# Row-tile pairs in seven products, and when a block's end is written, in a two-layer encoder trunk

## The chip, the cores and the metric

The kernel runs on one core of one Trainium2 chip. Times are device microseconds of that core, as the median of several executions; a profiled execution has a time of its own. The engines are TensorE (PE; its weight loads are listed apart as PEld), VectorE (DVE), ScalarE (ACT), GpSimd (POOL) and SyncE (SP), which issues most transfers.

## The reference

Two layers over 256 tokens of width 2048, all in float32:

```python
for l in range(DEPTH):
    h = rmsnorm(x, norm_g[l])
    proj = h @ w_in[l]                       # 2048 x 7168 columns
    a_x, a_b, a_c, a_g, d_q, d_k, d_v, d_g, m_q, m_g = jnp.split(proj, offsets, axis=-1)
    y_a = short_gated_conv(a_x, a_b, a_c, conv_w[l], conv_b[l]) * jax.nn.silu(a_g)
    q = rmsnorm(d_q.reshape(b, s, DIFF_HEADS, 2, DIFF_HALF_DIM), diff_q_norm_g[l])
    k = rmsnorm(d_k.reshape(b, s, DIFF_HEADS, 2, DIFF_HALF_DIM), diff_k_norm_g[l])
    ...                                      # differential attention, 6 heads, and its gate
    mkv = rmsnorm(mem, mem_norm_g[l]) @ w_mem_kv[l]   # 256 memory tokens, 2048 x 1024
    ...                                      # attention into the memory, 4 heads, and its gate
    x = x + jnp.concatenate([y_a, y_d, y_m], axis=-1) @ w_out[l]
```

Nearly all the arithmetic is in the three products with `w_in`, `w_mem_kv` and `w_out`.

## The kernel before

**Products in three parts.** Each float32 operand is held as a high part `hi`, rounded to the type that TensorE takes, and a low part `lo`, what is left. A product is hi·hi + hi·lo + lo·hi, so each pair of a 128-row tile of weights (512 columns) and a tile of 128 tokens is three matmuls of 512 columns (`products`, called from L282).

**Blocks and chunks.** `block` computes 512 columns of a product for both token tiles: 16 row tiles, taken two at a time. Such a chunk loads 512 KB of weights on SP's queue into one of four `raw` tiles, casts them to `hi` on ScalarE (L271), subtracts for `lo` on VectorE (L272), and does 12 matmuls. There are four `hi` and four `lo` tiles, so the splitting can run up to four chunks ahead of TensorE. After each chunk `run_side` is called: it counts chunks and advances by one step every task whose due time has come. `later(g, n)` makes a task due n chunks on; a number that a task yields is the chunks until its next step. All other work (norms, turns, attention heads, convolution) is written as such tasks.

**Order.** A planner orders the program before it runs: by the order in which instructions are written, but it lets a later one go first when an earlier one is not ready by its own cost estimates. Instructions passed to `keep_in_program_order` (`pin` for short) stay in written order among themselves on their engine. On the chip each engine takes its list strictly in order.

**Pairs.** `seven` replaces two row tiles by two token tiles by two neighbouring blocks, eight tile products, by seven, of three matmuls each. It needs sums and differences of the tokens (`token_sums`: one add of 512 columns, four of 128, a cast and a subtract for their parts) and of the weights (four subtracts, L357; casts and `lo` of seven half tiles, L354), and four banks for the products that are shared (`x`, from the pools `ps_s` and `ps_t`). `joint` runs a block with such pairs put between its chunks at given `places`; the pairs also start the sums `far` of the next block, which then lacks those row tiles and is `near`'s partner. `near` and `far` together take all four `acc` banks. `collect` (L1041, L1045) and `gather` (L1068) add the shared products to both. Layer 0 has a joint at block 3 (partner 4) with one pair, layer 1 at block 1 (partner 2) with one, and the products with `w_out` two and three pairs.

**The attention blocks.** Blocks 0 to 2 of `w_in`'s attention columns hold queries and keys, 3 to 5 values and gates. In layer 0 they come in this order, after the product with the memory; in layer 1 twelve row tiles of blocks 3 and 0 are done first, then the rest of both, then 1, 2, 4, 5. At the end of a query or key block `normed` runs at once: sums of squares on ScalarE for 16 groups (L413), the mean and the root on GpSimd (L414, L185), and 16 multiplies of 64 columns on ScalarE (L421), which free the `acc` banks. Eight chunks later a task turns the sheet (L451), carries it through scratch memory in eight transfers, and splits it into `yT` (L509 to L519).

**The memory keys.** `keep_keys` copies the raw keys out of their banks; the task `mem_keys` norms them, and `keys` stores them to scratch (L821) and loads them back (L822), both on GpSimd's queue, and turns them on VectorE into `mkT` (L824, pinned).

Of the kernel before, what the change touches and what calls it, by code (L numbers as in the profile page):

```python
# [11 lines left out]
F32R = mybir.dt.float32r  # L12
I32 = mybir.dt.int32
AF = mybir.ActivationFunctionType
ALU = mybir.AluOpType
# [25 lines left out]
BIG = 3.0e38  # L41

# [7 lines left out]
def encoder(ctx: ExitStack, tc: tile.TileContext, x, mem, norm_g, w_in, conv_w, conv_b,  # L50
# [351 lines left out]
    def col(st, which, t):  # L402
        return st[:, which, t:t + 1]

    def normed_steps(acc, gs, st, home):

        ng, w = NB // gs, gs // B
        ss = small.tile([P, NT, ng], F32, tag=f"ss{ng}", name=nm("ss"))
        r = small.tile([P, NT, ng], F32, tag=f"rs{ng}", name=nm("rs"))
        for t in range(NT):  # L410
            for g in range(ng):
                sq = small.tile([P, gs], F32, tag="sq", name=nm("sq"), bufs=1)
                nc.scalar.activation(sq, acc[t][:, g * gs:(g + 1) * gs], AF.Square, accum_out=ss[:, t, g:g + 1])  # L413
            nc.gpsimd.tensor_scalar(ss[:, t], ss[:, t], 1.0 / gs, col(st, ET, t), ALU.mult, ALU.add)  # L414
            rsqrt(r[:, t], ss[:, t])
            yield 1
        both = home()
        for t in range(NT):
            for g in range(ng):
                j, b = divmod(g * w, NA)  # L420
                nc.scalar.activation(both[:, b:b + w, j, t], strips(acc[t][:, g * gs:(g + 1) * gs]), AF.Copy,  # L421
                                     scale=r[:, t, g:g + 1])
            yield 1
        return both

    def normed(*how):
        steps = normed_steps(*how)
        try:
            while True:
                next(steps)  # L430
        except StopIteration as end:
            return end.value
# [67 lines left out]
    def qk_T(l, yT, nat, q, k):  # L500

        whole = yield from turn_sheet(nat)
# [153 lines left out]

    def mem_pair(l, n, st):
        heads = (2 * n, 2 * n + 1)
        es = []
        for h in heads:  # L660
            while held["e"] == 2:
                yield 1
            held["e"] += 1
            es.append((yield from mem_scores(l, h, st)))
            yield 2
        yield 4
# [142 lines left out]
    def mem_keys(l, kraw):  # L809

        nat = yield from normed_steps([kraw[:, t] for t in range(NT)], P, stm[0], sheets("v"))
        yield 6
        yield from keys(l, nat)

    def keys(l, nat):
# [7 lines left out]
        yield 8  # L823
# [8 lines left out]
    class Memory:  # L832
# [5 lines left out]
        def load(self, s):  # L838
            if s in self.raw or s in self.parts or s >= DEPTH * KT + KT // CK:
                return  # L840
            l, k = divmod(s, KT)
            self.raw[s] = raw_tile()
            if l == DEPTH:
                pin(nc.sync.dma_start(self.raw[s], x_row_tiles(w_in[0], k * CK)[:, :, C_D:C_D + NB]))
                return
# [169 lines left out]
    for l in range(DEPTH):  # L1015
# [17 lines left out]
        def joint(b, places, summed, home):  # L1033
# [18 lines left out]
            def pair_at(n):  # L1052
                def run(near):
                    rows = lambda k: x_row_tiles(w_in[l], k, 1)[:, 0, C_D + b * NB:C_D + (b + 2) * NB]
                    seven(xT, 2 * n, summed[n], rows, near, far, x, n == 0, n == len(places) - 1,
                          ((tmp, ("sh", "e")[n]),) * 2, lambda: None, ((tmp, "e"), (keep, "mga"))[l])
# [6 lines left out]
                    between={c: pair_at(n) for n, c in enumerate(places)})  # L1063
# [13 lines left out]
        near_b, far_b, places, tags, home = ((3, 4, (10,), ("bgx",), "bgT"), (1, 2, (8,), ("bgT",), "bgx"))[l]  # L1077
        far, summed = None, []
        for b in order:
            if l == 0 and b == near_b - 1:  # L1080
                summed = [x_sums(n, tags[n]) for n in range(len(places))]
            if b in begun:
                acc = x_block([(C_D + b * NB, NB)], ALLK[-QT:], acc=begun[b])
                if b == 3:
                    for n in range(len(places)):
                        summed.append(x_sums(n, tags[n]))
            elif b == near_b:
                acc, far, us = joint(b, places, summed, home)
                acc = gather(acc, us[0:2])
            elif b == far_b:  # L1090
                acc = x_block([(C_D + b * NB, NB)], ALLK[2 * len(places):], acc=far, opened=(True, False))
                acc = gather(acc, us[2:4])
            else:
                acc = x_block([(C_D + b * NB, NB)], ready=m.ready if l == 0 and b == order[0] else None)
# [10 lines left out]
            if b < 3:  # L1105
                tasks.append(later(qk_T(l, yT, normed(acc, HALF, st, sheets(("mqT", "mga", "e")[b])),
                                 (0, 0, 4) if b == 0 else (0, 4, 2) if b == 1 else None,
                                 (256, 0, 2) if b == 1 else (0, 2, 4) if b == 2 else None), 8))
            else:
                for t in range(NT):  # L1110
                    if b == 3:
                        nc.scalar.activation(v[:, t, 0:NB], acc[t], AF.Copy, scale=col(st, R, t))
                    elif b == 4:
                        nc.scalar.activation(v[:, t, NB:768], acc[t][:, 0:256], AF.Copy, scale=col(st, R, t))
                        silu2(ga[:, t, 0:256], acc[t][:, 256:512], st, t)
                    else:
                        silu2(ga[:, t, 256:768], acc[t], st, t)
# [5 lines left out]
        def turn_mq(nat):  # L1123
# [4 lines left out]
        tasks.append(later(turn_mq(normed(acc, P, st, sheets("bgx"))), 8))  # L1128
# [207 lines left out]
```

## Time and profile before

| | |
|---|---|
| median of 3 executions | 918.17 us (917.14 to 918.65) |
| the profiled execution | 920.46 us |
| its span, first to last instruction | 918.7 us |
| TensorE busy | 910.9 us (99%) |
| VectorE busy | 638.8 us (70%) |
| ScalarE busy | 589.0 us (64%) |
| GpSimd busy | 125.3 us (14%) |
| moved by transfers | 215.18 MB, 234 GB/s |

A group's row gives line, engine, operation, what is written from what, shape, count, then busy time in us, mean ns of one, and the idle time of the engine ahead of it with what ended it. A row of the timeline or of the chain begins with the start and the duration in us; in the timeline a bracket gives idle time and its releaser.

### The profile page before, as it was taken

Reading aid. Unit: us, or ns where it says so; the run is one execution under the profiler, and the core shown is the slowest. Engines: PE = TensorE matmul, PEld = TensorE weight load, DVE = VectorE, ACT = ScalarE, POOL = GpSimd, SP = SyncE. Lnnn points to the kernel's source line nnn. Section 1 sums busy time; section 2 is a strip of 40 time slices with the busy share of each in tenths; the row PEclk is TensorE's granted clock in tenths of the full one; section 3 lists DMA queues with packets and bytes.
Section 4 is the critical chain, followed back from the end, with each engine's and each line's share of the span. In section 5 each row is a group of like instructions: output and inputs, shape, how many; then the busy total and the mean of one; then the engine's idle time right before and its main releaser. Section 6 shows DMA issues by size and latency. Waiting matters only on the chain.

```text
span 918.7 us, 12662 instructions
## 1 busy us (share of the span) xinstructions
PE 910.9 (99%) x4203; PEld 752.3 (82%) x4203; DVE 638.8 (70%) x877; ACT 589.0 (64%) x1226; POOL 125.3 (14%) x187
## 2 busy tenths in 40 slices
PE   9999999999999999999999999999999999999998
PEld 6887787888888888888888888888888888888887
DVE  5557645677658658677689666667658678588786
ACT  6679776757767656545557558787667666546352
POOL 2376142200031010000000202221032010000000
PEclk9999999999999999999999999999999999999999
DMA  8898777876777989978776874988768998968842
GB/s 288 284 266 252 236 227 226 255 215 221 222 212 205 256 228 262 265 234 246 254 228 226 259 251 130 277 241 238 223 183 230 266 271 248 271 206 241 281 154 92
DMA packets 244051, 215.18 MB, mean 234 GB/s; under 512 B 131977, under 2 KB 171721, under 8 KB 243985
## 3 DMA queue, kind: packets, MB, share of 16 engines
q1 hardware_dynamic: 239008, 208.71, 76.1%
q0 software_dynamic: 3776, 4.59, 1.9%
q10 hardware_dynamic: 1200, 1.07, 0.3%
q8 instruction: 33, 0.54, 0.2%
q14 instruction: 34, 0.27, 0.1%
HBM read 193.30 MB, written 21.00 MB: 233 GB/s over the span
## 4 chain that ended last, share of the span: by engine, by line
PE 88%; DMA 5%; ACT 2%; DVE 2%; POOL 2%; issue 1%; DVEq 0%; ACTq 0%; POOLq 0%
PE acc L282 80%; PE x L328 2%; DMA raw<-in_w_mem_kv_dram 2%; DMA raw<-in_w_in_dram 2%; PE acc L328 2%; PE po L489 1%; PE s L579 1%; DMA sh<-kd 1%; DVE lo L869 1%; PE po L706 1%; DVE xf L743 1%; ACT hi L271 1%; ACT sq L413 1%; POOL rs L185 1%; ACT sh L421 0%
## 5 line engine op out<-in xcount | busy, mean ns | idle before, releaser
L282 PE MATMUL acc<-hi,xT 128*128 128x512 f32 x1760 | 550.4, 390 | 0.0
L272 DVE TENSOR_TENSOR lo<-raw,hi 128x1024 fp32r<-128x1024 f32 x266 | 323.6, 1221 | 171.0 <-ACT hi L271 166.1
L271 ACT CAST hi<-raw 128x1024 fp32r<-128x1024 f32 x266 | 278.4, 1052 | 189.0 <-PE acc L282 138.2
L282 PEld LDWEIGHTS acc<-hi,xT 128*128 128x128 f32 x1760 | 330.3, 188 | 68.6
L282 PE MATMUL acc<-lo,xT 128*128 128x512 f32 x880 | 343.1, 390 | 2.0 <-DVE lo L272 1.6
L282 PEld LDWEIGHTS acc<-lo,xT 128*128 128x128 f32 x880 | 165.2, 188 | 36.3 <-DVE lo L272 2.0
L282 PE MATMUL acc<-hi,yT 128*128 128x512 f32 (+1 forms) x432 | 134.2, 388 | 0.0
L282 PEld LDWEIGHTS acc<-hi,yT 128*128 128x128 f32 x432 | 81.0, 188 | 16.7
L282 PE MATMUL acc<-lo,yT 128*128 128x512 f32 x216 | 83.7, 388 | 0.0
L282 PE MATMUL acc<-hi,memT 128*128 128x512 f32 x248 | 78.7, 393 | 0.0
L869 DVE SCALAR_TENSOR_TENSOR lo<-raw,cva,hi 128x1024 fp32r<-128x1024 f32 (+1 forms) x34 | 40.7, 1218 | 24.8 <-ACT hi L868 24.8
L282 PEld LDWEIGHTS acc<-hi,memT 128*128 128x128 f32 x248 | 46.1, 188 | 9.5
L282 PE MATMUL acc<-lo,memT 128*128 128x512 f32 x124 | 48.6, 392 | 0.7 <-DVE lo L869 0.7
L282 PEld LDWEIGHTS acc<-lo,yT 128*128 128x128 f32 x216 | 40.6, 188 | 8.4
L868 ACT ACTIVATE hi<-raw,cva 128x1024 fp32r<-128x1024 f32 (+1 forms) x34 | 36.5, 1098 | 7.6 <-DMA raw<-in_w_mem_kv_dram 7.0
L354 ACT CAST hi<-wide 128x1024 fp32r<-128x1024 f32 x21 | 22.0, 1056 | 18.1 <-DVE wide L357 7.4
L185 POOL TENSOR_TENSOR rs<-ss,root 128x8 f32<-128x8 f32 (+1 forms) x20 | 31.7, 1583 | 1.7
L354 DVE TENSOR_TENSOR lo<-wide,hi 128x1024 fp32r<-128x1024 f32 x21 | 25.4, 1221 | 8.4 <-ACT hi L354 8.2
L414 POOL TENSOR_SCALAR ss<-ss,st 128x8 f32<-128x8 f32 (+1 forms) x16 | 10.5, 654 | 137.4 <-ACT sq L413 137.4
L282 PEld LDWEIGHTS acc<-lo,memT 128*128 128x128 f32 x124 | 23.3, 188 | 6.6 <-DVE lo L869 1.8
L596 ACT ACTIVATE e<-e,mx 128x256 f32<-128x256 f32 x48 | 23.8, 497 | 6.7 <-DVE mx L591 6.0
L394 POOL TENSOR_SCALAR stt<-ssum 128x2 f32<-128x2 f32 x3 | 1.5, 507 | 187.3 <-DVE ssum L770 187.3
(207 smaller groups left out, 858.6 us busy)
## 6 DMA issues: line engine op xcount, KB each, us to landing
raw<-in_w_in_dram SPq DMA_DIRECT2D x188, 512.0 KB, 4.9
raw<-in_w_out_dram SPq DMA_DIRECT2D x54, 512.0 KB, 4.6
raw<-in_w_in_dram SPq DMA_DIRECT2D x64, 256.0 KB, 4.1
raw<-in_w_mem_kv_dram SPq DMA_DIRECT2D x30, 512.0 KB, 6.1
d<-sh SPq DMA_DIRECT2D x88, 128.0 KB, 4.4
sh<-d SPq DMA_DIRECT2D x72, 128.0 KB, 3.8
wide<-in_w_out_dram SPq DMA_DIRECT2D x10, 512.0 KB, 5.9
xs<-in_x_dram SPq DMA_DIRECT2D x4, 512.0 KB, 6.5
```

The source lines that it names most:

```text
L185: nc.gpsimd.tensor_tensor(r, t, root[:, 0:n], ALU.pow)
L271: nc.scalar.copy(hi, raw)
L272: nc.vector.tensor_tensor(lo_, raw, hi.bitcast(F32), ALU.subtract)
L282: i = nc.tensor.matmul(acc, left, right, start=start, stop=stop)
L328: nc.tensor.matmul(acc, left[a], right[b], start=first and i == 0, stop=last and i == 2)
L354: return ((hi, pin(nc.scalar.copy(hi, src))), (lo, pin(nc.vector.tensor_tensor(lo, src, hi.bitcast(F32), ALU.subtract))))
L413: nc.scalar.activation(sq, acc[t][:, g * gs:(g + 1) * gs], AF.Square, accum_out=ss[:, t, g:g + 1])
L414: nc.gpsimd.tensor_scalar(ss[:, t], ss[:, t], 1.0 / gs, col(st, ET, t), ALU.mult, ALU.add)
L489: nc.tensor.matmul(po[:, t, :], eT[:, i, t, k, :], v[:, k, h * P:(h + 1) * P], start=k == 0, stop=k == NT - 1)
L596: nc.scalar.activation(e[:, c, i], e[:, c, i], AF.Exp, bias=mx[:, c, i:i + 1], scale=-1.0, accum_out=sm[:, c, i:i + 1])
L868: both = (nc.scalar.activation(hi[:, j], raw[:, j], AF.Copy, scale=g), nc.vector.scalar_tensor_tensor(lo[:, j], raw[:, j], g, hi[:, j].bit ...
L869: nc.vector.scalar_tensor_tensor(lo[:, j], raw[:, j], g, hi[:, j].bitcast(F32), ALU.mult, ALU.subtract))
```

## The change

- `normed_steps` does its squares in steps of four groups for the 64-wide heads, and its multiplies as one VectorE `tensor_tensor` for each token tile, with the factor broadcast, in place of 16 (or 4) on ScalarE. `normed` is gone: the norms of blocks 0 to 2 and of the memory queries are steps of a task.
- The ends of the six attention blocks (norm, or copies and gates, and `gather` ahead of them) are tasks due two chunks after their block.
- Layer 0 has two joints, at blocks 1 and 3, with two pairs each at places 4, 8 and 6, 10; layer 1 has one, at block 1, with two pairs at 6, 10. The pairs' landing places and the tile for the first half tile's parts are set for each pair.
- The token sums stand in row tiles 12 to 15 of `yT`, which the memory heads fill later, and are made by a task during block 0 (layer 0) or after block 3 (layer 1).
- The memory keys' chain waits 5 chunks for 6 ahead of its store, but its norm's steps are two chunks longer; the turn is 11 chunks after the load for 8. Layer 0's sheet is in tile `bgT`, layer 1's in `v` as before.
- The second pair of memory heads waits until the first has its scores; FIRST is 0 and changes nothing.

```diff
@@ normed_steps
                 nc.scalar.activation(sq, acc[t][:, g * gs:(g + 1) * gs], AF.Square, accum_out=ss[:, t, g:g + 1])
+                if g % 4 == 3 and g + 1 < ng:
+                    yield 1
...
         for t in range(NT):
-            for g in range(ng):
-                j, b = divmod(g * w, NA)
-                nc.scalar.activation(both[:, b:b + w, j, t], strips(acc[t][:, g * gs:(g + 1) * gs]), AF.Copy,
-                                     scale=r[:, t, g:g + 1])
-            yield 1
+            to = both[:, :, :, t].rearrange("p (g b) j c -> p j g b c", b=w)
+            of = acc[t].rearrange("p (j g b c) -> p j g b c", g=NA // w, b=w, c=B)
+            nc.vector.tensor_tensor(to, of, r[:, t].rearrange("p (j g) -> p j g", g=NA // w).unsqueeze(3).unsqueeze(4)
+                                    .to_broadcast([P, NB // P, NA // w, w, B]), ALU.mult)
+            yield 2
@@ qk_T
-    def qk_T(l, yT, nat, q, k):
+    def qk_T(l, yT, get, st, home, q, k):
+        nat = yield from normed_steps(get(), HALF, st, home)
         whole = yield from turn_sheet(nat)
@@ mem_pair
+        while n > 0 and (l, n - 1) not in begun_pairs:
+            yield 1
@@ mem_keys, keys
-        nat = yield from normed_steps([kraw[:, t] for t in range(NT)], P, stm[0], sheets("v"))
-        yield 6
+        nat = yield from normed_steps([kraw[:, t] for t in range(NT)], P, stm[0], sheets(("bgT", "v")[l]))
+        yield 5
         yield from keys(l, nat)
...
-        yield 8
+        yield 11
@@ the layer's loop
-        def x_sums(n, tag):
-            home = keep.tile([P, 2, 4, P], F32R, tag=tag, name=nm("sums"))
-            for _ in token_sums(xT, 2 * n, home):
-                pass
-            return home
+        def x_sums(n):
+            home = yT[:, :, KT - QT + 2 * n:KT - QT + 2 * (n + 1)].rearrange("p two k (h r) -> p two (k h) r", r=P)
+            summed.append(home)
+            yield from token_sums(xT, 2 * n, home)
...
-        near_b, far_b, places, tags, home = ((3, 4, (10,), ("bgx",), "bgT"), (1, 2, (8,), ("bgT",), "bgx"))[l]
+        turned, raw, late = ((tmp, "sh"),) * 2, ((tmp, "e"),) * 2, ((keep, "v"), (keep, "ga"))
+        mga, bgx = (keep, "mga"), (keep, "bgx")
+        joints = ({1: ((4, 8), (turned, raw), (mga,) * 2, "bgT"), 3: ((6, 10), (late, turned), (bgx,) * 2, "bgT")} if l == 0
+                  else {1: ((6, 10), (raw, turned), (mga,) * 2, "bgx")})
...
+            if l == 0 and b == 0:
+                tasks.append(later(all_x_sums(), 1))
+            finish = None
             if b in begun:
                 acc = x_block([(C_D + b * NB, NB)], ALLK[-QT:], acc=begun[b])
                 if b == 3:
-                    for n in range(len(places)):
-                        summed.append(x_sums(n, tags[n]))
-            elif b == near_b:
-                acc, far, us = joint(b, places, summed, home)
-                acc = gather(acc, us[0:2])
+                    tasks.append(later(all_x_sums(), 1))
+            elif b in joints:
+                places = joints[b][0]
+                acc, far, us = joint(b, *joints[b])
+                finish = us[0:2]
...
+            def sums_of(acc=acc, us=finish):
+                return gather(acc, us) if us else acc
...
-                tasks.append(later(qk_T(l, yT, normed(acc, HALF, st, sheets(("mqT", "mga", "e")[b])),
+                tasks.append(later(qk_T(l, yT, sums_of, st, sheets(("mqT", "mga", "e")[b]),
...
-                                 (256, 0, 2) if b == 1 else (0, 2, 4) if b == 2 else None), 8))
+                                 (256, 0, 2) if b == 1 else (0, 2, 4) if b == 2 else None), 2))
...
+                tasks.append(later(leave(b, sums_of, v, ga), 2))
...
-        tasks.append(later(turn_mq(normed(acc, P, st, sheets("bgx"))), 8))
+        tasks.append(later(turn_mq(normed_steps(acc, P, st, sheets("bgx"))), 0))
```

More of the change, by code (lines that the diff above doesn't have):

```diff
@@ L41 @@
 BIG = 3.0e38
+FIRST = 0
 C_X, C_B, C_C, C_G = 0, 768, 1536, 2304
@@ L665, in mem_pair @@
             yield 2
+        begun_pairs.add((l, n))
         yield 4
@@ L838, in load @@
         def load(self, s):
-            if s in self.raw or s in self.parts or s >= DEPTH * KT + KT // CK:
+            if s in self.raw or s in self.parts or s >= DEPTH * KT + (KT - FIRST) // CK:
                 return
@@ L843, in load @@
             if l == DEPTH:
-                pin(nc.sync.dma_start(self.raw[s], x_row_tiles(w_in[0], k * CK)[:, :, C_D:C_D + NB]))
+                pin(nc.sync.dma_start(self.raw[s], x_row_tiles(w_in[0], FIRST + k * CK)[:, :, C_D:C_D + NB]))
                 return
@@ L1025, in x_block, with joint @@
             return block(xT, w_in[l], cols, order, rows=x_row_tiles, **how)
[L1027 to L1033 removed]
+        def x_sums(n):
+            home = yT[:, :, KT - QT + 2 * n:KT - QT + 2 * (n + 1)].rearrange("p two k (h r) -> p two (k h) r", r=P)
+            summed.append(home)
+            yield from token_sums(xT, 2 * n, home)
+        def joint(b, places, homes, singles, home, **how):
             near, far = accumulators(), accumulators()
@@ L1062, in joint @@
             x_block([(C_D + b * NB, NB)], ALLK[2 * len(places):], acc=near, opened=(False, False),
-                    between={c: pair_at(n) for n, c in enumerate(places)})
+                    between={c: pair_at(n) for n, c in enumerate(places)}, **how)
             return near, far, us
@@ L1076, in encoder, with all_x_sums @@
         begun = {b: x_block([(C_D + b * NB, NB)], ALLK[:-QT], more=True) for b in order[:2]} if l > 0 else {}
-        near_b, far_b, places, tags, home = ((3, 4, (10,), ("bgx",), "bgT"), (1, 2, (8,), ("bgT",), "bgx"))[l]
+        turned, raw, late = ((tmp, "sh"),) * 2, ((tmp, "e"),) * 2, ((keep, "v"), (keep, "ga"))
+        mga, bgx = (keep, "mga"), (keep, "bgx")
+        joints = ({1: ((4, 8), (turned, raw), (mga,) * 2, "bgT"), 3: ((6, 10), (late, turned), (bgx,) * 2, "bgT")} if l == 0
+                  else {1: ((6, 10), (raw, turned), (mga,) * 2, "bgx")})
         far, summed = None, []
+        def all_x_sums():
+            for n in range(2):
+                yield from x_sums(n)
+                yield 1
         for b in order:
-            if l == 0 and b == near_b - 1:
-                summed = [x_sums(n, tags[n]) for n in range(len(places))]
+            if l == 0 and b == 0:
+                tasks.append(later(all_x_sums(), 1))
+            finish = None
             if b in begun:
@@ L1121, in encoder, with turn_mq @@
         acc = x_block([(C_M, NB)])
-        def turn_mq(nat):
+        def turn_mq(steps):
+            nat = yield from steps
+            yield 1
             yield from turn_sheet(nat, mqT)
```

35 lines of the change are left out of this document (16 added, 19 removed).

## The prediction

> **What bounds the kernel now.** I read the page first: shares of busy time, then the chain that ended last.
>
> ```profile
> span 918.7 us, 12662 instructions
> PE 910.9 (99%) x4203; PEld 752.3 (82%) x4203; DVE 638.8 (70%) x877; ACT 589.0 (64%) x1226; POOL 125.3 (14%) x187
> PE 88%; DMA 5%; ACT 2%; DVE 2%; POOL 2%; issue 1%; DVEq 0%; ACTq 0%; POOLq 0%
> ```
>
> TensorE is busy all the time and is 88% of the chain. A busy TensorE can still run slowly, so I looked at the pace next, in the chain in order of time:
>
> ```profile
> 403.77 65.32 PE acc L282 x288
> ```
>
> 65.32 us for 288 matmuls of 512 columns is 0.227 us each. The 390 ns that the groups give as the mean of one is overlapped time; a matmul that goes away is worth 0.227 us. Then TensorE's waits, and its timeline around the three stops on VectorE's `lo`:
>
> ```profile
> PE acc L282 <- DVE lo L272: 1.6, 1, 1.6
> PE acc L282 <- DVE lo L869: 0.7, 2, 0.5
> PE acc L282 <- DVE lo L861: 0.5, 1, 0.5
> ...
> 100.99 0.84 PE L282 MATMUL acc<-hi,xT 128*128 128x512 f32 x3
> 102.29 0.50 PE L282 MATMUL acc<-lo,xT 128*128 128x512 f32 x1 [0.46 <-DVE lo L861]
> 104.47 0.84 PE L282 MATMUL acc<-hi,xT 128*128 128x512 f32 x3
> 105.33 0.50 PE L282 MATMUL acc<-lo,xT 128*128 128x512 f32 x1
> 148.31 0.61 PE L282 MATMUL acc<-hi,xT 128*128 128x512 f32 x2
> 150.48 0.50 PE L282 MATMUL acc<-lo,xT 128*128 128x512 f32 x1 [1.56 <-DVE lo L272]
> ```
>
> By start times: three matmuls from 100.99 should be followed at 101.67, and the next starts at 102.29 (0.62 lost); from 104.47 at 105.15, and it is 105.33 (0.18); two from 148.31 at 148.76, and it is 150.48 (1.72). Each restart takes 0.50 where a running matmul takes 0.39, another 0.11 each. Together 2.85 us. VectorE's timeline tells whose fault that is:
>
> ```profile
> 99.88 1.25 DVE L824 STREAM_TRANSPOSE mkT<-sh 128x1024 f32<-128x1024 f32 x1 [4.76 <-DMA sh<-kd]
> ...
> 141.21 0.29 DVE L339 TENSOR_TENSOR sums<-sums,f 128x128 f32<-128x128 f32 x1
> 147.87 1.25 DVE L824 STREAM_TRANSPOSE mkT<-sh 128x1024 f32<-128x1024 f32 x1 [6.38 <-DMA sh<-kd]
> ```
>
> Both times the turn of the memory keys (L824) stood at the head of VectorE's queue before its load had landed. The `lo` halves of the weights were queued behind it, and TensorE ran through its stock.
>
> **The change, part by part.** *Pairs.* A row-tile pair does 21 matmuls in place of 24. There were one joint block with one pair in each layer; now layer 0 has two joints of two pairs and layer 1 one of two: 6 for 2, four more, 4 x 3 x 0.227 = 2.72 us less on TensorE, wherever it is fed.
>
> *What a pair costs VectorE.* Rows of the groups by shape:
>
> ```profile
> L272 DVE TENSOR_TENSOR lo<-raw,hi 128x1024 fp32r<-128x1024 f32 x266 | 323.6, 1221 | 171.0 <-ACT hi L271 166.1 <-DMA raw<-in_w_in_dram 1.5 <-DMA sh<-d 1.2
> L357 DVE TENSOR_TENSOR wide<-wide 128x512 f32<-128x512 f32 x14 | 9.7, 692 | 0.5
> L354 DVE TENSOR_TENSOR one<-wide,one 128x512 fp32r<-128x512 f32 x7 | 4.8, 684 | 2.0 <-ACT one L354 2.0
> L1068 DVE TENSOR_TENSOR u<-acc,u 128x512 f32<-128x512 f32 x8 | 5.2, 675 | 0.0
> L421 ACT ACTIVATE sh<-acc,rs 128x64 f32<-128x64 f32 x64 | 14.5, 335 | 5.0 <-POOL rs L185 5.0
> L343 DVE TENSOR_TENSOR sums<-sums,sums 128x512 fp32r<-128x512 f32 x7 | 4.8, 685 | 0.9 <-ACT sums L342 0.9
> ```
>
> A pair asks 0.68 (`one`) + 3 x 1.22 (as long as L272's) + 4 x 0.69 (differences) = 7.1 us of VectorE; the two chunks that it replaces ask 2 x 1.22 = 2.44. So each new pair is 4.7 us more for VectorE while TensorE's share falls from 5.46 to 4.77. ScalarE gets three half-size casts more, and the loads move the same 1 MB on SP's queue in two transfers of 512 KB, so neither sets anything new.
>
> *Layer 0's window.* Three of the four new pairs fall between the first x block and the fourth, so I summed VectorE there, and beside it the two nearest rows, layer 1's joint and the end of the last product with three pairs:
>
> ```profile
> 98.50:207.00 108.50, 106.46 (x466) 86.85 (x465) 68.84 (x68) 76.98 (x220) 21.04 (x21) 1.00 0.77 230
> 876.00:899.00 23.00, 23.00 (x103) 18.89 (x102) 22.08 (x24) 14.70 (x17) 0.00 (x0) 1.00 0.38 121
> 553.00:583.00 30.00, 30.00 (x133) 24.74 (x132) 22.18 (x24) 23.04 (x75) 5.98 (x6) 1.00 0.54 162
> ```
>
> (The fields are length, then busy time of TensorE, its weight loads, VectorE, ScalarE, GpSimd.) VectorE had 68.8 us. To come: 3 pairs x 4.7 = 14.0; a second `collect`, four adds of the kind of L1068, 2.7; four more `gather` adds, 2.7; eight norm multiplies that leave ScalarE, 8 x 0.69 = 5.5; one more set of token sums, 2.4 (L343's split and an add of its size at 0.68 each, four quarter-size adds like L339's at 0.28). That is 96.1 us. TensorE will want 108.5 - 3 x 0.68 - 2.85 = 103.6 us for the same blocks: VectorE at 93%, with 7.5 us to lose. The three pairs at 876 to 899 ran at 22.08 of 23.0, 96%, and TensorE was busy for all 23.0. So a stretch this dense can be fed if the stock is full at its start. What the one pair of layer 0 lost itself is in TensorE's timeline:
>
> ```profile
> 182.62 0.39 PE L328 MATMUL acc<-hi,sums 128*128 128x512 f32 x1
> 182.98 0.50 PE L328 MATMUL acc<-hi,xT 128*128 128x512 f32 x1
> ```
>
> 0.36 between two starts, 0.13 too much, and 0.11 for the restart: 0.24. I charge each of layer 0's three new pairs with that, 0.7 us in all, and layer 1's with nothing, where VectorE goes from 22.2 to 22.2 + 4.7 + 1.4 = 28.3 of 29.3. The bounds are 0, as at 876, and what VectorE would run over if its waits stayed:
>
> ```profile
> DVE lo L272 <- ACT hi L271: 17.8, 12, 3.2
> DVE mkT L824 <- DMA sh<-kd: 11.1, 2, 6.4
> DVE yT L519 <- ACT yT L518: 2.7, 1, 2.7
> DVE lo L354 <- ACT hi L354: 2.4, 1, 2.4
> DVE one L354 <- ACT one L354: 2.0, 1, 2.0
> DVE lo L861 <- ACT hi L861: 2.0, 2, 1.5
> DVE yT L510 <- ACT yT L509: 1.8, 1, 1.8
> DVE xT L757 <- ACT xT L756: 1.2, 1, 1.2
> DVE sums L343 <- ACT sums L342: 0.9, 1, 0.9
> ```
>
> Without the keys' 11.1 and the 17.8 behind ScalarE's casts these are 13.0 us. If all remained, and ScalarE's 5.0 us behind `rs` (L421 above) came over with the multiplies, VectorE would need 96.1 + 18.0 = 114.1 us, 10.5 too many. I take the low end, because most of the 13.0 are waits on a ScalarE that loses the small L421 of three blocks here, 3 x 16 x 0.335 = 16 us, against some 5 us of new casts.
>
> *The keys' chain.* In steps of a chunk (12 matmuls, 2.73 us), the first store to scratch moves from 10 to 11 after the chain's first step and the turn from 8 to 11 behind the load's issue. POOL's store and load go one chunk later, the turn four. Three chunks more between load and turn are 8.2 us, against waits of 4.76 and 6.38. So L824 should find its data, and the 2.85 us go. What was behind it (`lo`) runs straight on; what waits for mkT, the memory heads, comes long after. The `v` tile is held until then, 147.87 + 4 x 2.73 = 158.8, and the first pair of the second joint wants it as a landing place. That pair reaches TensorE at about 98.5 + 21.9 + 25.9 + 16.4 + 8.2 = 170.9 (a whole block, a joint of six chunks and two pairs, its partner's six chunks, three chunks more), 12 us later: nothing, or up to 1 us if the load of some 6 us is crowded. Bounds: all of it, or nothing if the load moves as far as the turn.
>
> *Block ends.* The squares and multiplies are written two chunks later and in smaller steps, so the casts for the next chunks go first. They now hand the banks over late, and a joint's `far` sums need two banks of the block before. ScalarE's and GpSimd's rows for the first block's end (it ended at 98.5 + 21.9 = 120.4) give the times:
>
> ```profile
> 124.93 1.64 POOL L185 TENSOR_TENSOR rs<-ss,root 128x8 f32<-128x8 f32 x1
> 127.69 1.16 ACT L421 ACTIVATE sh<-acc,rs 128x64 f32<-128x64 f32 x5
> ```
>
> Before, the first bank was free at 128.85. Now one VectorE multiply behind `rs` frees it at 126.57 + 0.7 = 127.3; the first joint's first pair starts two chunks after 120.4, at 125.9, and asks for it as its third product, six matmuls on, at 127.2. If the multiply comes no sooner than the old eight plus two chunks, 134.3, the pair does its other six products first (4.1 us) and TensorE stands 134.3 - 125.9 - 4.1 = 4.3 us. I take nothing: VectorE reaches it as soon as `rs` lands unless it is behind.
>
> The query and key turns go from 8 to 10 chunks behind their block, with their eight scratch transfers on SP. Tightest is layer 1, where the first keys' split and the first scores stand so:
>
> ```profile
> 614.85 0.74 DVE L519 SCALAR_TENSOR_TENSOR yT<-sh,kgain,yT 128x512 fp32r<-128x512 f32 x1
> 622.42 1.62 PE s L579 x24
> ```
>
> Two chunks later is 621.1, still ahead of 622.4. If it is later yet, x blocks fill TensorE: nothing; the whole pair would slip by a chunk. The token sums' new home, the guard in the memory pairs, FIRST = 0 and the memory queries' steps issue nothing new on the path.
>
> *A rule to weigh.* TensorE's weight loads are busy 82%, its matmuls 99%. The Trainium skill, Perfetto Trace Analysis, section Identifying the Most-Contended Engine, holds matmul busy time to be a bad measure of headroom and weight-load busy time a good one; by that TensorE would have 18% of slack, and the 2.72 us might be absorbed. The trace disagrees where the pace is 0.227 us over 288 matmuls with no wait in between.
>
> **The sum.** The profiled execution took 920.46 us, 918.7 of span and 1.8 around it; it lies 2.3 over the median of 918.17. 920.46 - 2.72 - 2.85 + 0.7 = 915.6, which stands to a median of 913.3.
>
> **Rivals.**
> - *VectorE becomes the bound in layer 0.* Place: 98 to 207. From 7.5 us of waits on, each further one is a microsecond of TensorE. With the 18.0 above: 918.2 - 2.7 - 2.85 + 10.5 = 923.1, and with some 2 us of stock at the start (it was used up at 102 and is refilled) 921. For it: 93%, and every wait on `rs` now stands in VectorE's queue. Against it: 96% without a stop at 876. Slower.
> - *Late banks.* 4.3 us in the first joint and that less one chunk (2.7), 1.6, in layer 1's, whose first pair stands a chunk further on: 913.3 + 5.9 = 919.2. For it: the order written. Against it: the multiply is one instruction, and free to run early.
> - *The keys' waits only move.* 913.3 + 2.85 = 916.2. Against it: 8.2 us exceed both waits.
> - *The matmuls saved are absorbed.* 913.3 + 2.72 = 916.0. The pace speaks against it.
> - *Cleaner than I charge.* No loss at the pairs, and the 0.7 behind L869 gone as well, since ScalarE's small multiplies ahead of it go: 911.9.
>
> **How the numbers follow.** Forecast 0.54 (its own range 912.4 to 915.6), cleaner 0.08, keys 0.08, absorbed 0.04, late banks 0.15, VectorE 0.11. No change that can be told is within 0.2%, 916.3 to 920.0. Faster gets the first two and most of the next two, 0.70; the same the rest of those and the banks, 0.19; slower 0.11. The range leaves out the VectorE rival above and the best part of the cleaner case below: 911.7 to 919.4.
>
> **What would show it.** 12 fewer matmuls of 512 columns; L328 with 231 matmuls for 147; L824 without idle time ahead of it and no TensorE stop at 102 or 150; twenty VectorE multiplies of some 0.69 us where L421 was. VectorE near 96 us in layer 0's window. Wrong if TensorE's waits list shows more than 3 us behind `lo` of L354 or L272, or behind a multiply that frees a bank.

## The result and the profile after

The changed kernel takes 923.29 us (median of four, 923.03 to 923.83) against 917.78 for the kernel before on the same chip (917.14 to 918.65): a ratio of 1.006, 95% interval 1.0043 to 1.0078. It is slower; 913.3 had been forecast. The profiled execution took 923.83 us. Line numbers after the change are one higher (the matmul of the blocks is L283, ScalarE's cast L272, VectorE's subtraction L273, the pair's half tiles L355, its differences L358, its matmuls L329); the new multiply is L424, the sum of squares L414, the mean L417, the root `rs` L186.

The head of the page and the chain by engine, after:

```profile
span 922.0 us, 12596 instructions
PE 911.0 (99%) x4191; PEld 750.4 (81%) x4191; DVE 677.4 (73%) x941; ACT 567.9 (62%) x1109; POOL 125.4 (14%) x187
PE 83%; ACT 4%; DVE 3%; POOL 3%; DMA 3%; issue 2%; SPq 1%; DVEq 0%; POOLq 0%; ACTq 0%
```

TensorE does 12 matmuls fewer, as forecast, and its busy time is the same: busy time doesn't show a lost microsecond here. The chain does: TensorE's share fell from 88% to 83%, and ScalarE, VectorE and GpSimd together went from 6% to 10%. So I went to what TensorE waited for, and to VectorE's wait behind GpSimd (what waited and for whom; us in total, times, longest):

```profile
PE acc L329 <- DVE lo L355: 2.2, 2, 1.5
PE acc L283 <- DVE lo L273: 1.7, 2, 1.3
...
PE acc L329 <- ACT hi L355: 1.0, 2, 0.6
PE s L635 <- ACT parts L629: 0.7, 1, 0.7
PE acc L329 <- DVE sh L424: 0.3, 1, 0.3
```

```profile
DVE sh L424 <- POOL rs L186: 19.0, 16, 1.9
```

The waits behind the memory keys are gone from the list. In their place are waits inside the pairs. Sixteen of the twenty multiplies stood at the head of VectorE's queue without their `rs`, 19.0 us in all. Six of these waits, 6.8 us, lie at the joints' first pairs; behind the ten others, 12.2 us, TensorE's list shows no stop. VectorE's timeline in layer 0's first pair shows what that does:

```profile
123.13 1.22 DVE L355 TENSOR_TENSOR lo<-wide,hi 128x1024 fp32r<-128x1024 f32 x1
124.39 0.69 DVE L358 TENSOR_TENSOR wide<-wide,wide 128x512 f32<-128x512 f32 x1
126.64 0.69 DVE L424 TENSOR_TENSOR sh<-acc,rs 128x512 f32<-128x512 f32 x1 [1.56 <-POOL rs L186]
127.25 0.68 DVE L358 TENSOR_TENSOR wide<-wide 128x512 f32<-128x512 f32 x1
127.85 2.42 DVE L355 TENSOR_TENSOR lo<-wide,hi 128x1024 fp32r<-128x1024 f32 x2
131.84 0.69 DVE L424 TENSOR_TENSOR sh<-acc,rs 128x512 f32<-128x512 f32 x1 [1.56 <-POOL rs L186]
132.44 2.35 DVE L273 TENSOR_TENSOR lo<-raw,hi 128x1024 fp32r<-128x1024 f32 x2
```

The multiply of block 0's first token tile stands between the third and the fourth difference of the pair. VectorE reaches it at 125.08 and stands until 126.64; the last difference and two `lo` come behind it. The second multiply stands ahead of the next chunk's `lo`, and costs the same 1.56 us. GpSimd works off the two ends one after the other:

```profile
124.58 2.03 POOL L186 TENSOR_TENSOR rs<-ss,root 128x8 f32<-128x8 f32 x1
...
127.30 1.82 POOL L417 TENSOR_SCALAR ss<-ss,st 128x8 f32<-128x8 f32 x1
129.21 2.59 POOL L186 TENSOR_TENSOR rs<-ss,root 128x8 f32<-128x8 f32 x1
```

TensorE's rows for the first pair, and then for the second joint's:

```profile
127.39 0.49 PE L329 MATMUL acc<-hi,yT 128*128 128x512 f32 x1 [0.33 <-DVE sh L424]
129.06 0.50 PE L329 MATMUL acc<-hi,xT 128*128 128x512 f32 x1 [0.49 <-ACT hi L355]
133.71 0.50 PE L283 MATMUL acc<-lo,xT 128*128 128x512 f32 x1 [1.30 <-DVE lo L273]
...
179.97 0.50 PE L329 MATMUL acc<-lo,xT 128*128 128x512 f32 x1 [1.47 <-DVE lo L355]
```

The stop at 127.39 is the far bank that the multiply hands over; at 129.06 ScalarE's cast had waited for the late difference; at 133.71 `lo` came late behind the second multiply. In the other two joints the first multiply waits only 0.2 us, and the second has the same picture in VectorE's timeline (at 178 and at 564, the latter in layer 1):

```profile
178.08 0.69 DVE L424 TENSOR_TENSOR sh<-u,rs 128x512 f32<-128x512 f32 x1 [1.53 <-POOL rs L186]
178.69 1.22 DVE L355 TENSOR_TENSOR lo<-wide,hi 128x1024 fp32r<-128x1024 f32 x1
...
564.29 0.69 DVE L424 TENSOR_TENSOR sh<-acc,rs 128x512 f32<-128x512 f32 x1 [1.82 <-POOL rs L186]
564.90 1.22 DVE L355 TENSOR_TENSOR lo<-wide,hi 128x1024 fp32r<-128x1024 f32 x1
```

To add such stops up I took, for each two matmuls that follow one another, the time between their starts less the pace of that shape (0.227 us for 512 columns). Between 120 and 200 us and between 560 and 580, where the three joints lie, that excess is 8.1 us here. It was 2.2 in the profile of before, of which 1.8 us (the stop at 148.5 with its restart) lay behind the memory keys. I call it "the joints' excess" below.

### The profile page after: what moved, and what is told of

It is laid out like the page before. It is cut to its first block, busy times and chain, and to the rows that moved or that the text cites. A ratio compares the mean times of both kernels' runs of the same rounds, so it can differ in the third digit from the quotient of the medians.

```text
span 922.0 us, 12596 instructions
## 1 busy us (share of the span) xinstructions
PE 911.0 (99%) x4191; PEld 750.4 (81%) x4191; DVE 677.4 (73%) x941; ACT 567.9 (62%) x1109; POOL 125.4 (14%) x187
## 4 chain that ended last, share of the span: by engine, by line
PE 83%; ACT 4%; DVE 3%; POOL 3%; DMA 3%; issue 2%; SPq 1%; DVEq 0%; POOLq 0%; ACTq 0%
PE acc L283 75%; PE x L329 2%; PE acc L329 2%; ACT sq L414 2%; DVE lo L273 1%; DMA raw<-in_w_in_dram 1%; POOL rs L186 1%; DMA d<-sh 1%; POOL ss L417 1%; SPq L467 1%; PE s L575 1%; ACT hi L272 1%; PE po L484 1%; PE po L707 1%; PE acc L887 1%
## 5 line engine op out<-in xcount | busy, mean ns | idle before, releaser
L283 PE MATMUL acc<-hi,xT 128*128 128x512 f32 x1696 | 532.0, 390 | 0.0
L273 DVE TENSOR_TENSOR lo<-raw,hi 128x1024 fp32r<-128x1024 f32 x258 | 314.0, 1222 | 138.1 <-ACT hi L272 133.3
L272 ACT CAST hi<-raw 128x1024 fp32r<-128x1024 f32 x258 | 269.4, 1049 | 204.1 <-PE acc L283 144.7
L283 PEld LDWEIGHTS acc<-hi,xT 128*128 128x128 f32 x1696 | 318.2, 188 | 66.0
L283 PE MATMUL acc<-lo,xT 128*128 128x512 f32 x848 | 330.7, 390 | 1.7 <-DVE lo L273 1.7
L283 PEld LDWEIGHTS acc<-lo,xT 128*128 128x128 f32 x848 | 159.2, 188 | 34.8 <-DVE lo L273 2.9
L283 PE MATMUL acc<-hi,yT 128*128 128x512 f32 (+1 forms) x432 | 134.3, 388 | 0.0
L283 PEld LDWEIGHTS acc<-hi,yT 128*128 128x128 f32 x432 | 81.0, 188 | 16.8
L283 PE MATMUL acc<-lo,yT 128*128 128x512 f32 x216 | 83.7, 388 | 0.0
L283 PE MATMUL acc<-hi,memT 128*128 128x512 f32 x248 | 78.5, 392 | 0.0
L355 ACT CAST hi<-wide 128x1024 fp32r<-128x1024 f32 x33 | 34.4, 1047 | 39.7 <-DVE wide L358 29.0
L283 PEld LDWEIGHTS acc<-hi,memT 128*128 128x128 f32 x248 | 46.2, 188 | 9.4
L283 PE MATMUL acc<-lo,memT 128*128 128x512 f32 x124 | 48.4, 390 | 0.0
L283 PEld LDWEIGHTS acc<-lo,yT 128*128 128x128 f32 x216 | 40.5, 188 | 8.4
L355 DVE TENSOR_TENSOR lo<-wide,hi 128x1024 fp32r<-128x1024 f32 x33 | 40.1, 1220 | 3.8 <-ACT hi L355 3.4
L186 POOL TENSOR_TENSOR rs<-ss,root 128x8 f32<-128x8 f32 (+1 forms) x20 | 32.9, 1646 | 1.7
L417 POOL TENSOR_SCALAR ss<-ss,st 128x8 f32<-128x8 f32 (+1 forms) x16 | 13.9, 866 | 130.7 <-ACT sq L414 130.6
L283 PEld LDWEIGHTS acc<-lo,memT 128*128 128x128 f32 x124 | 23.3, 188 | 5.0 <-DVE lo L870 0.2
(213 smaller groups left out, 915.1 us busy)
```

The costliest lines, as they stand in the source:

```text
L186: nc.gpsimd.tensor_tensor(r, t, root[:, 0:n], ALU.pow)
L272: nc.scalar.copy(hi, raw)
L273: nc.vector.tensor_tensor(lo_, raw, hi.bitcast(F32), ALU.subtract)
L283: i = nc.tensor.matmul(acc, left, right, start=start, stop=stop)
L355: return ((hi, pin(nc.scalar.copy(hi, src))), (lo, pin(nc.vector.tensor_tensor(lo, src, hi.bitcast(F32), ALU.subtract))))
```

## The experiments

Three theories were open when the first runs went off. **Waits**: the multiplies wait for `rs` inside the pairs, and the pair's work stands behind them in VectorE's order. **Load**: VectorE has more work there than time, wherever the multiplies stand. **Late banks**: the `acc` banks come free two chunks later, and the joint's far sums wait. All the times, with the ratio to the kernel before on the same chip, and the joints' excess of the profiled execution:

| kernel | median, us | ratio, 95% interval | joints' excess, us |
|---|---|---|---|
| before, two more executions profiled | 918.01; 918.19 | | 0.4; 1.1 |
| changed | 923.29 | 1.0060 (1.0043 to 1.0078) | 8.1 |
| changed, a second time | 923.24 | 1.0050 (1.0037 to 1.0064) | 7.7 |
| changed, pairs as before | 918.70 | 0.9997 (0.9989 to 1.0006) | 0.4 |
| changed, multiplies on ScalarE | 923.07 | 1.0048 (1.0033 to 1.0062) | 7.6 |
| changed, multiplies kept in order | 917.33 | 0.9986 (0.9977 to 0.9995) | 2.1 |
| changed, factor from a constant | 915.95 | 0.9967 (0.9954 to 0.9979) | 0.9 |
| changed, pairs later | 921.99 | 1.0034 (1.0022 to 1.0046) | 6.9 |
| kept in order, first joint later | 917.17 | 0.9979 (0.9967 to 0.9991) | 1.5 |
| kept in order, all pairs later | 916.83 | 0.9978 (0.9966 to 0.9990) | 1.0 |
| before, with the keys' chain later | 917.46 | 0.9990 (0.9981 to 0.9999) | 0.4 |

The kernel before had medians of 919.14, 919.05 and 918.89 in the three sets of runs.

### The pairs as before

```diff
-        joints = ({1: ((4, 8), (turned, raw), (mga,) * 2, "bgT"), 3: ((6, 10), (late, turned), (bgx,) * 2, "bgT")} if l == 0
-                  else {1: ((6, 10), (raw, turned), (mga,) * 2, "bgx")})
+        joints = ({3: ((10,), (turned,), ((tmp, "e"),), "bgT")} if l == 0 else {1: ((8,), (turned,), (mga,), "bgx")})
...
-            for n in range(2):
+            for n in range(1):
                 yield from x_sums(n)
```

> The changed kernel with the pairs of before: one joint of one pair in each layer, all else as changed (token sums in yT, late block ends, late keys, multiplies on VectorE). 2.7 us more of matmuls than the changed kernel. W: the multiplies still wait, but away from most pairs VectorE has slack to lose it in; L: no crowded stretch is left. Both: the stops at 127 to 134 and 174 to 182 us go, 923.3 + 2.7 - 7 = 919. If the late block ends or the late keys cost time of themselves, it stays over 921.

918.70, a ratio of 0.9997. Everything but the new pairs and their set of token sums (late block ends, multiplies on VectorE, keys, the sums' new place) together does nothing that can be measured, and the whole loss is in the pairs and what meets them. VectorE still waits for `rs` here, 8.4 us in seven waits, with 0.4 us of excess at the joints: it isn't the wait alone that costs, but a wait with due work behind it.

### The multiplies kept in the order of the program

```diff
-            nc.vector.tensor_tensor(to, of, r[:, t].rearrange(...)...to_broadcast(...), ALU.mult)
+            pin(nc.vector.tensor_tensor(to, of, r[:, t].rearrange(...)...to_broadcast(...), ALU.mult))
```

> The changed kernel with the norm's multiplies held in the written order on VectorE, one edit. In VectorE's list both multiplies of layer 0's block 0 then stand behind the whole second pair, where they stood inside and behind the first. VectorE's work is the same to the instruction. W: the waits on GpSimd's factors go from VectorE (19 us in 16 waits to under 5), and the stops behind them: 918 to 920. L: the work is the same, so the stops stay: near 923. B: the banks come ten microseconds later, the far sums wait: 925 or more.

917.33, a ratio of 0.9986: one word turns 0.5 or 0.6% slower into 0.1% faster. In VectorE's list both multiplies of block 0 now stand behind the second pair. The waits behind `rs`, VectorE's timeline in the same pair, and the window from 98 to 215 us of this kernel (fields as in the prediction):

```profile
DVE sh L424 <- POOL rs L186: 4.3, 4, 1.3
```

```profile
124.85 0.69 DVE L358 TENSOR_TENSOR wide<-wide 128x512 f32<-128x512 f32 x1
125.46 1.22 DVE L355 TENSOR_TENSOR lo<-wide,hi 128x1024 fp32r<-128x1024 f32 x1
...
138.52 0.68 DVE L424 TENSOR_TENSOR sh<-acc,rs 128x512 f32<-128x512 f32 x1
```

```profile
98.00:215.00 117.00, 116.44 (x524) 94.45 (x523) 102.28 (x129) 81.00 (x191) 24.36 (x23) 1.00 0.76 237
```

The same window of the changed kernel, and the one that the prediction summed:

```profile
98.00:215.00 117.00, 112.50 (x504) 90.66 (x503) 99.12 (x115) 77.99 (x183) 27.95 (x21) 1.00 0.72 229
97.90:207.00 109.10, 104.59 (x453) 84.17 (x452) 92.91 (x108) 72.64 (x175) 27.95 (x21) 1.00 0.70 224
```

VectorE does more in the same time when it isn't held up (102.3 us for 99.1), and TensorE is busy for 116.4 of 117.0. Load falls: the work fits. Late banks falls as a price of microseconds: the multiply comes at 138.5, 12 us later than in the changed kernel, and none of TensorE's waits names it. TensorE had done all the other products of both pairs first; the six matmuls of both pairs that need the far bank start at 139.84, 0.6 us behind its end.

### The multiplies on ScalarE again

```diff
-            to = both[:, :, :, t].rearrange("p (g b) j c -> p j g b c", b=w)
...
-            nc.vector.tensor_tensor(...)
+            for g in range(ng):
+                j, b = divmod(g * w, NA)
+                nc.scalar.activation(both[:, b:b + w, j, t], strips(acc[t][:, g * gs:(g + 1) * gs]), AF.Copy,
+                                     scale=r[:, t, g:g + 1])
             yield 2
```

> The changed kernel with the norm's multiplies back on ScalarE (16 or 4 of them for each token tile), all else as changed. Theory W (VectorE stops at the multiplies because their factors come late from GpSimd, and the pair's differences and lo halves stand behind them): those stops go, TensorE's waits at 133.7, 180.0, 182.2 and 566 us go with them, 4 to 5 us: near 918.5. Theory L (VectorE's sheer work for the pairs is too much where they stand): VectorE loses 5.5 of some 96 us in layer 0's window, its stops at the first pair of each joint stay, 1 to 2 us gained: near 921.5. Theory B (the far sums wait for banks that are handed over late): 16 small multiplies free a bank later than one large one: no gain or slower, 923 to 925.

923.07: a miss for Waits as I had put it, since VectorE no longer waits for `rs` and nothing is won. The waits of VectorE (first two rows) and of ScalarE (the third) in this kernel:

```profile
DVE lo L355 <- ACT hi L355: 10.9, 8, 2.8
DVE one L355 <- ACT one L355: 10.3, 3, 4.9
```

```profile
ACT sh L424 <- POOL rs L186: 12.2, 14, 3.8
```

The wait has moved with the multiplies, and ScalarE spends 2 us on each token tile's eight multiplies, with the pair's casts in the same queue; VectorE stands behind ScalarE. In the first joint the largest stop, 2.03 us, is of the kind that Late banks had named: the multiplies on ScalarE waited 0.86 us for `rs` (at 128.22), and gave the far bank free only at 130.2. With the slow pace behind it, told at the end, this stop makes 3.9 of the 7.6 us. In the second joint TensorE's stops (0.71 and 0.56 us the largest) are behind ScalarE's casts, mostly where ScalarE was busy and not waiting. So this run shows that the multiplies do harm on ScalarE too, and doesn't decide between the theories.

### The factor from a constant

```diff
-            nc.vector.tensor_tensor(to, of, r[:, t].rearrange(...)
+            nc.vector.tensor_tensor(to, of, root[:, 0:ng].rearrange(...)
```

> The changed kernel, with the factor of the twenty norm multiplies taken from a constant column in place of rs: it leaves out the scaling by the head norm (GpSimd still works rs out, and nothing waits for it). The multiplies stay inside the joints' first pairs in VectorE's list, and VectorE's work stays 93 us of 109 in layer 0's window. Waits theory (the multiplies wait for GpSimd's rs with the pair's differences behind them): the stops of some 6 us at the first pairs go, since nothing is waited for, and the time is that of the pinned kernel, 917.3, in 916.5 to 918.5. Load theory (VectorE has too much work there): 923, as its work is the same. Late banks: the multiplies are still written two chunks after the block's end, the far bank stop at 126.7 was 0.5 us: 922.5.

915.95, a ratio of 0.9967; a little under the range given. VectorE's work is the same. Against what was expected, the multiplies do not all stay inside the pairs. In the first joint both do, each one place earlier than in the changed kernel; in the second both now stand ahead of the pair, and in layer 1's the first does, while the second stands inside it. So the first joint is the clean comparison. VectorE's timeline there, VectorE in the second joint, and TensorE's largest wait at a pair:

```profile
125.31 0.68 DVE L424 TENSOR_TENSOR sh<-acc,root 128x512 f32<-128x512 f32 x1
125.91 0.68 DVE L358 TENSOR_TENSOR wide<-wide,wide 128x512 f32<-128x512 f32 x1
...
127.23 1.22 DVE L355 TENSOR_TENSOR lo<-wide,hi 128x1024 fp32r<-128x1024 f32 x1
128.37 0.68 DVE L424 TENSOR_TENSOR sh<-acc,root 128x512 f32<-128x512 f32 x1
```

```profile
165.67 1.28 DVE L424 TENSOR_TENSOR sh<-u,root 128x512 f32<-128x512 f32 x2
167.67 0.69 DVE L355 TENSOR_TENSOR one<-wide,one 128x512 fp32r<-128x512 f32 x1 [0.72 <-ACT one L355]
```

```profile
PE acc L329 <- ACT hi L355: 0.4, 1, 0.4
```

With two multiplies inside the first joint's pair, the excess there is about 1 us, where the changed kernel has 3: the multiplies' 0.68 us each cost TensorE at most what is left, and the wait is what costs. With 8.1 us of excess in all joints down to 0.9, the span went from 922.0 to 915.1, 6.9 us.

### The pairs later, without and with the order kept

The first run moves the pairs of all joints to places 8 and 10; the second does that with the multiplies pinned; the third is pinned and moves the first joint's pairs alone, to 6 and 10.

```diff
-        joints = ({1: ((4, 8), (turned, raw), (mga,) * 2, "bgT"), 3: ((6, 10), (late, turned), (bgx,) * 2, "bgT")} if l == 0
-                  else {1: ((6, 10), (raw, turned), (mga,) * 2, "bgx")})
+        joints = ({1: ((8, 10), (turned, raw), (mga,) * 2, "bgT"), 3: ((8, 10), (late, turned), (bgx,) * 2, "bgT")} if l == 0
+                  else {1: ((8, 10), (raw, turned), (mga,) * 2, "bgx")})
```

> The changed kernel, multiplies not pinned, with the pairs of all three joints at places 8 and 10, so that the first pair starts four chunks (10.9 us) behind the end of the block and not two (5.5 us) or three. Waits theory: the first multiply has its rs before the pair comes (it landed at 126.6, the pair would start at about 131.4), the second (rs at 131.8) still stands inside the pair; about half of the 6 us of stops stays: 919 to 921. Load theory: the same work, with only one chunk between the two pairs: 923 or later. Late banks: the bank is free long before, 922.8.

921.99, 1 us over the range expected. The mechanism is the expected one: the first multiply of each joint finds its `rs` (it doesn't wait at 125.61, 170.96 and 557.29), and the planner puts the second inside the pair again, where it stands for 1.5 to 1.8 us. The joints' excess is 6.9 us for 8.1, and 1.6 of these are matmuls at half pace behind the longest stop (told at the end); without them the time would be some 920.4, inside the range. VectorE in the second joint of this kernel, GpSimd's end of that `rs`, and TensorE behind it:

```profile
176.36 0.69 DVE L424 TENSOR_TENSOR sh<-u,rs 128x512 f32<-128x512 f32 x1 [1.53 <-POOL rs L186]
176.97 0.68 DVE L358 TENSOR_TENSOR wide<-wide 128x512 f32<-128x512 f32 x1
```

```profile
174.25 2.08 POOL L186 TENSOR_TENSOR rs<-ss,root 128x8 f32<-128x8 f32 x1
```

```profile
178.84 0.50 PE L329 MATMUL acc<-hi,xT 128*128 128x512 f32 x1 [1.90 <-ACT hi L355]
```

> The multiplies kept in the order of the program, and the pairs of all three joints at places 8 and 10: four chunks behind the block's end, with only one chunk between the two pairs. Waits theory: a multiply comes ahead of the first pair in VectorE's list with its rs landed 4 us before; nothing of GpSimd's is waited for inside a pair, and ScalarE is done with the squares: 916.5 to 917.5, unless one chunk is too little for VectorE to get ahead of the second pair, 918 to 919. Load theory (two pairs of 4.7 us of VectorE in 2 x 4.8 + 2.7 us of TensorE is what decides): slower than the pinned kernel by 1 us or more in each joint, 920. Late banks: 917.3 or less, since the bank is free earlier against the pair.

916.83, a ratio of 0.9978. The wait for ScalarE's `hi` is the only one at a pair that is left, 0.7 us:

```profile
PE acc L329 <- ACT hi L355: 0.7, 1, 0.7
```

One chunk between the pairs is enough for VectorE, which Load had denied. With the order kept, the pairs can stand later; without it, later is no cure.

> The multiplies of the changed kernel kept in the order of the program (behind the second pair), and the first joint's pairs at places 6 and 10 in place of 4 and 8. Waits theory: the stop of 0.5 us at 126.4 that is left in the pinned kernel comes from ScalarE, which has the block's squares and its own wait for token sums ahead of the pair's casts; a chunk more lets it finish, and the time is 916.5 to 917.2. If what is left is no matter of ScalarE's queue: 917.3, as in the pinned kernel. Load theory: the same work, 917.3 or later. Late banks: the multiplies stay behind the second pair, which comes a chunk later, so the banks of the block come free later too: 917.3 plus 1 to 3 us.

917.17, a ratio of 0.9979. The stop of 0.5 us in the first joint is gone in its profile, as expected, but the second joint has 1.5 us of its own, where the pinned kernel has 0.3, and the interval overlaps with those of the two other pinned kernels. Which of the three is best can't be told here. Each beats both kernels: the one with all pairs later is 0.9978 (0.9966 to 0.9990) of before, and 923.24 for the changed kernel against 916.83 is 0.7% more.

### The changed kernel and the kernel before once more

> The changed kernel itself once more. Waits theory: the stops at the joints' first pairs are set by the order of VectorE's list, so they come back at the same places (126.7, 128.2, 131.9, 175.7, 178.1, 181.5, 565.1, each within 0.3 us of its size) and the time is 922 to 924. If they belonged to one execution, as the stops at 102, 105 and 149 of the kernel before seem to: other places, other sizes.

The seven stops come back at the same places, 0.50, 0.65, 1.51, 0.69, 1.64, 0.54 and 0.83 us for 0.50, 0.66, 1.55, 0.73, 1.64, 0.52 and 0.84. They belong to the program. The stop at `parts` (L629, 0.7) does not come back.

> The kernel before, unchanged, profiled a second time. Its first profile lay 2.3 us over its median, and the changed kernel is 5.5 us slower by the medians but only 3.3 us longer by the two spans. Theory: the 2.85 us that the first profile showed behind the memory keys' turn are not there in most executions; then this profile's span is near 916 us and TensorE's stops at 102 and 149 us are shorter or gone. Rival: they are always there, and the 2.3 us lie around the span; then the span is near 918.5 again.

> The kernel before, a third profile. If the stops of 2.85 us behind the memory keys' turn were a trait of the first profiled execution: no stop at 102, 105 and 149, TensorE some 7.5 us over its pace in all, span near 916. If they are typical and the second profile was the exception: 2.85 us of stops there and a span near 918.7.

The stops at 102 and 105 are in neither of the two executions; that at 149 is there once, at 0.63 for 1.72 us. The turn of the keys in the first of the two, and the only wait for `lo` that TensorE has in that execution (it lies at 77.91, ahead of both turns):

```profile
98.85 1.25 DVE L824 STREAM_TRANSPOSE mkT<-sh 128x1024 f32<-128x1024 f32 x1 [3.05 <-DMA sh<-kd]
...
145.47 1.25 DVE L824 STREAM_TRANSPOSE mkT<-sh 128x1024 f32<-128x1024 f32 x1 [4.66 <-DMA sh<-kd]
```

```profile
PE acc L282 <- DVE lo L869: 0.6, 1, 0.6
```

VectorE still waits 3.05 and 4.66 us for the load, 1.7 us less each time than in the profile that I had read, and the stock of split weights covers that. The spans are 916.2 and 916.4 for 918.7.

### The keys' chain alone

```diff
         nat = yield from normed_steps([kraw[:, t] for t in range(NT)], P, stm[0], sheets("v"))
-        yield 6
+        yield 7
         yield from keys(l, nat)
...
-        yield 8
+        yield 11
         tc.keep_in_program_order(nc.vector.transpose(
```

> The kernel before, with only the memory keys' chain later (first store after step 7 of its count and not 6, the turn 11 steps behind the load and not 8). By the term of the prediction: 2.85 us less, a ratio of 0.997. If those stops are not there in most executions: a ratio of 1.000 within 0.001.

0.9990 (0.9981 to 0.9999), between the two answers: some 0.9 us (0.1 to 1.7), not 2.85. The wait itself is gone, as the group of both turns shows, whose last field is the idle time ahead of it:

```profile
L824 DVE STREAM_TRANSPOSE mkT<-sh 128x1024 f32<-128x1024 f32 x2 | 2.5, 1238 | 0.0
```

## Why the prediction was wrong, point by point

Forecast 913.3, measured 923.29: 10.0 us apart. Two terms make some 8.5 of them, the keys' (2.0) and the pairs' (6.5). Another 0.5 us lies in layer 1's attention, at about 680 to 700 us, where every kernel with the change loses that much more than the kernel before over the same matmuls; no run looked into it. The rest is open.

- **The keys' 2.85 us, and the 2.3 between profile and median.** The mechanism was right (the later turn waits for nothing), the size was not. The sum took 2.85 us of stops from an execution that was 2.3 us over the median, and then subtracted those 2.3 us as well. But the median, 918.17, is that of executions which mostly lack these stops: two others show 0 and 0.63 us of them. The same microseconds were counted twice. From the median the keys could give about 0.9 us, and the error of this term is some 2 us.
- **The pairs' +0.7 us, and "I take the low end" for VectorE's waits.** This is the larger term: the joints' excess came out at 7.7 to 8.1 us, where two typical executions of before had 0.4 and 1.1, so some 7.2 us for 0.7. The failing sentence is "VectorE reaches it as soon as `rs` lands unless it is behind". The opposite held: VectorE was there first, by 1.5 to 1.8 us at four of the six multiplies in the joints, and everything behind the multiply waited with it. The first joint's first multiply did come when the prediction said (126.64, for 126.57); what it held up had been left out. The upper bound took 5.0 us of waits on `rs` over from ScalarE; they came to 19.0. The prediction costed the multiply by its 0.69 us and asked when its result was wanted. It didn't ask where the planner would put it, and what stood behind it there. The edit added a wait, and the list of what is queued behind it was the step that was left out.
- **The rival "VectorE becomes the bound"** priced its outcome at 923.1, or 921 with some stock, and gave the wait on `rs` in VectorE's queue as its sign. The sign came true and the time was near; the reason was another. It wanted VectorE to run out of time at 93%, and the pinned kernel does all the work with 2.1 us of excess. That the time came out near its price is luck. Its chance of 0.11 was too low all the same, since one of its two conditions, a wait in an order that is strictly kept, could be read from the code.
- **Late banks** had a price of 4.3 us in the first joint, and cost 0.5 there (2.03 with the multiplies on ScalarE). The order written was no guide: the planner moves the multiply earlier into the pair, and where it is held late, TensorE's other products move ahead.
- **The matmuls saved are absorbed** fell, by the kernel with the constant factor: 915.95 against 919.05 is 3.1 us less (1.9 to 4.2 by the interval), next to the 2.72 worked out from the pace and some 0.9 for the keys. The three pinned kernels, 1.8, 1.9 and 2.2 us less with 1.0 to 2.1 us of excess left, fit that, but wouldn't settle it alone.
- **VectorE's load** was forecast at 96.1 us for the window, and 92.9 were done in 109.1 us. The layer-1 joint, charged with nothing at 28.3 of 29.3 us, lost 1.4 us, again behind a multiply (564.29).
- **What would show it wrong** was set at more than 3 us of TensorE's waits behind `lo` of L354 and L272, or behind a multiply that frees a bank: they are 2.2 + 1.7 + 0.3 = 4.2.

The balance: a typical span of before is 916.3; less 2.72 for the matmuls, plus about 7.2 for the joints (8.1 and 7.7 less 0.4 to 1.1), is 920.8; the two spans of the changed kernel are 922.0, with 0.9 us of `parts` that came once, and 920.9. The cause, a wait for GpSimd inside the pair, is shown from two sides: by taking the wait away (in the first joint with the multiplies still inside the pair), and by moving the multiplies behind the pairs with GpSimd's work as it was. Why the planner thought the place free isn't shown: its estimates are in no trace.

## What to carry to other kernels

When work moves to another engine, don't cost it by its duration alone: find what it waits for, where it will stand in that engine's fixed order, and what is behind it there. A 0.69 us multiply cost TensorE 1.1 to 2.2 us each time that it stood in front of work that was due (0.50 + 0.66, 1.55, 1.64 + 0.54, 0.83 + 0.25). A planner's own order is safe only as far as its estimates are; where an operation waits for a long chain on other engines, fix its place behind the urgent work by hand. And take a stop as a gain to be had only if a second profiled execution shows it, most of all when the first lies above the median.

## What the hardware showed

**TensorE's clock after a stop.** In the kernel with the multiplies on ScalarE the far bank came 2.03 us late, and some matmuls after it ran at about half pace. Its rows of TensorE, and the granted clock (third field from the end) from 130 to 135 us:

```profile
127.79 0.40 PE L329 MATMUL acc<-hi,xT 128*128 128x512 f32 x1
130.22 0.49 PE L329 MATMUL acc<-hi,yT 128*128 128x512 f32 x1 [2.03 <-ACT sh L424]
...
131.72 0.63 PE L329 MATMUL x<-hi,yT 128*128 128x512 f32 x1
132.15 0.63 PE L329 MATMUL acc<-hi,xT 128*128 128x512 f32 x1
```

```profile
130.00:135.00 5.00, 4.78 (x14) 3.87 (x15) 3.41 (x3) 4.86 (x10) 2.34 (x2) 0.67 0.29 101
```

Starts are 0.43 us apart for 0.227, eight times (131.72 to 135.12), 1.6 us lost on top of the stop. The kernel with the pairs later has the same behind its 1.90 us wait at 178.84. By their starts these two stops are 2.20 and 2.06 us; one of 1.72 in the profile of before and those of up to 1.64 in the changed kernel did not bring it on. The Trainium skill, TensorE: Matmul & The Clock Gate, section Why this matters for your kernels, asks for no idle gaps over some 3 us between bursts of matmuls. Here some 2 us were enough, twice, so the measurement is stricter than the page; where the limit lies, two cases can't tell.

**GpSimd's small operations were longer where VectorE ran.** The mean of 128 x 8 elements (L417) took 0.27 us in the pinned kernel when VectorE happened to stand still, and 1.82 in the changed kernel (at 127.30 above), where VectorE ran throughout. The two rows of the pinned kernel:

```profile
123.10 1.14 POOL L417 TENSOR_SCALAR ss<-ss,st 128x8 f32<-128x8 f32 x1 [5.94 <-ACT sq L414]
...
127.04 0.27 POOL L417 TENSOR_SCALAR ss<-ss,st 128x8 f32<-128x8 f32 x1
```

VectorE worked during 97% of the first and during none of the second. Over all 13 profiles, the 50 of 156 such rows that overlap with no work of VectorE's took 0.26 to 0.28 us, and the 49 that overlap for 95% or more took 0.26 to 1.84, half of them over 1.1. The `rs` behind it took 1.64 to 2.63 us, and 1.64 to 1.67 in all 20 rows without overlap; but some long ones had VectorE at work for less than half of their time (2.03 us at 124.58 above). So the engine that waits for `rs` may itself have made it late. That is read from where the rows overlap; no run tested it.
